# Down projection of a SwiGLU layer on one core: another order of seven- and eight-product pairs, other pieces with their low parts added by DMA, and more lead

## The chip, the cores and the metric

One core of one Trainium2 chip runs the whole layer as one program. The metric is the device time of that program in microseconds (us); lower is better. What a measurement of this kernel can tell from no change is about 0.5%, or 1.45 us.

## The reference

One decoder layer in float32 for 256 tokens of width 1024. Only its last part matters here:

```python
h = rms_norm(x, norm2_g[l])
x = x + (jax.nn.silu(h @ w_gate[l]) * (h @ w_up[l])) @ w_down[l]
```

`w_gate` and `w_up` are 1024 x 2816, `w_down` is 2816 x 1024. Ahead of it stand the input projection, attention over 256 tokens, a causal convolution with its norm, and the output projection.

## The kernel before

**Products in parts.** TensorE multiplies in the rounded type fp32r. To keep float32 accuracy the kernel splits every operand into a high part (the value rounded to fp32r) and a low part (value minus high part), and adds up three products: high by high, low by high, high by low. Each weight therefore needs two preparing steps after it has been loaded. ScalarE copies it into the tile `wh` with rounding (line 265). The low part `wl` comes in one of two ways, in the helper `low_part` (lines 213 to 219): VectorE subtracts (line 219), or, for the pieces in the list `BY_DMA`, ScalarE writes the negated high part into `wl` (line 216) and a DMA issued by GpSimd adds the weight to it from memory (line 217).

**Pieces, blocks and places.** Weights are loaded by SyncE as blocks of 128 x 2048 (1 MB, tiles `raw`, line 196). There are four buffers for blocks. Half a block is a piece of 128 x 1024. There are eight places for pieces (`WGT = 8`, each place one `wh` and one `wl`); a new piece takes the place that holds the piece with the lowest number. The next block is loaded when the last reader of a block in its buffer is through: for ordinary blocks after the low part of their second piece, for the blocks of the down projection as told below.

**Lead.** The program is written out in one order, with `step()` calls that let side tasks emit their next instructions. Every engine takes its instructions strictly in that order. At each point `feed(upto)` (line 252) emits the copies up to one piece beyond `upto`, and the low parts up to `upto`, where `upto` is the piece now being multiplied plus a lead. The lead is `LEAD = 4`, and 5 from piece `FAR = 46` on and in the whole down projection. Copies are emitted in the order `turns`, which is by number but for the pieces in `BEHIND`: `BEHIND = {75: 72, ...}` puts the copy of piece 75 right behind that of piece 72.

**Gate and up.** Pieces 28 to 71 hold `w_gate` and `w_up`, two pieces for each of 22 groups `f` of 128 columns (tiles `fg` and `fu`, lines 292 and 294). `glu_task` computes silu(gate) times up for each group on ScalarE and VectorE and makes the activations for the down projection.

**Down.** The 22 groups make 11 pairs. A pair is a product of (2 x 2 blocks of activations) by (2 x 2 blocks of weights of 128 x 512). A pair marked F in the string `PAIRS` is done with seven block products after Strassen and Winograd, a pair marked P (plain) with eight. The products go to banks named `sum` (line 932, in the helper `add`). A fast pair has three pieces: the first is taken from its block as it is, the second and third are sums of its weights, which VectorE makes with three additions (lines 234 to 236, tiles `t`; the second piece needs the first of them, the third needs all). Its first quarter block is used alone, too: `single` (line 244) splits it with a copy on ScalarE (line 200) and a subtraction on VectorE (line 201), in the tiles `b11h` and `b11l` for every other fast pair and in `other` for the ones between and for the last. `single` of a pair is emitted at the start of the pair ahead of it, and asks for the block four further on. The products with that quarter (`M1`) stand third in a pair, and first in the last fast pair. A plain pair has two pieces, and its block is free after the copies, or, where VectorE makes the low parts, after these. Down pieces have the numbers 72 to 101, blocks the numbers 36 to 46, one for each pair.

The loop over pairs (lines 958 to 975) does pairs 0 to 9 in order; the last pair is done at the end, bank by bank, with the output (lines 1001 to 1009).

Of the kernel before, what the change touches and what calls it, by code (L numbers as in the profile page):

```python
# [36 lines left out]
LEAD = 4  # L37
# [20 lines left out]
V_PIECE = 21  # L58
SS_WAIT = 2
OUT_LATE = 6  # L60
PAIRS = "FFPFFPFFFFP"
FAST = [p for p in range(NF // 2) if PAIRS[p] == "F"]
PLAIN = [p for p in range(NF // 2) if PAIRS[p] == "P"]
DOWN = 72
BEHIND = {75: 72, 78: 74, 83: 79, 86: 82, 88: 85, 94: 90, 97: 93}
BY_DMA = [*range(45, DOWN, 3), 71, *BEHIND]
FAR = 46
SUMS = {66: 0, 69: 1}
FORMS_LATE = 11
# [72 lines left out]
def _build(nc, tc, t, ctx):  # L142
# [10 lines left out]
    def mm_bank(name, cols=512):  # L153
        return psum.tile([P, cols], F32, name=name, tag="mm", bufs=4)

    def t_bank(name, tag="t"):
        return psum.tile([P, 512], F32, name=name, tag=tag, bufs=2)
# [30 lines left out]
    def load_block(i, between=None):  # L188
        if i >= NB:
            return  # L190
        r = raw.tile([P, BW], F32, name=f"raw{i}", tag="raw")
        n = BW // (2 if between else 1)
        for j in range(BW // n):
            if j:
                between()
            nc.sync.dma_start(r[:, j * n:(j + 1) * n], t["w"][i - 2][:, j * n:(j + 1) * n])
        blocks[i] = r
# [5 lines left out]
    def new_piece():  # L203
        j = turns[len(pieces)]
        z = places.index(min(places))
        places[z] = j
        pieces[j] = [wgt.tile([P, PIECE], F32R, name=f"w{s}{j}", tag=f"w{s}{z}") for s in "hl"]
        i, a = divmod(j * PIECE, BW)
        if j >= DOWN:
            return pieces[j], down_piece(*down[j - DOWN]), j  # L210
        return pieces[j], blocks[i][:, a:a + PIECE] if i > 1 else None, j

    def low_part(dst, src, by_dma=False):

        if by_dma:
            nc.scalar.activation(dst[1], dst[0].bitcast(F32), AF.Copy, scale=-1.0)  # L216
            nc.gpsimd.dma_start(dst[1], src.bitcast(F32R), accum_op=ALU.add)  # L217
        else:
            nc.vector.tensor_tensor(dst[1], src, dst[0].bitcast(F32), op=ALU.subtract)  # L219
# [5 lines left out]
    index = {d: DOWN + a for a, d in enumerate(down)}  # L225
    turns = sorted(range(DOWN + len(down)), key=lambda j: BEHIND[j] + 0.5 if j in BEHIND else j)
    wsums, b11 = {}, {}
# [19 lines left out]
    def home(j):  # L247

        i, a = divmod(j * PIECE, BW)
        if j >= DOWN:  # L250
            p, a = down[j - DOWN]
            i, a = DOWN // 2 + p, (a if p in PLAIN else 1) * PIECE
        return t["w"][i - 2][:, a:a + PIECE]
# [7 lines left out]
    def feed(upto, more=1):  # L261
        last = DOWN + len(down) - 1
        while len(pieces) <= min(upto + more, last):
            dst, src, j = new_piece()
            nc.scalar.activation(dst[0], src, AF.Copy)  # L265
            if j in BY_DMA:
                low_part(dst, home(j), True)
            waiting.append((dst, src, j))
            waiting.sort(key=lambda w: w[2])
        while waiting and waiting[0][2] <= upto:  # L270
            dst, src, j = waiting.pop(0)
            if j not in BY_DMA:
                low_part(dst, src)
            if j < DOWN and j % 2:
                load_block(j // 2 + RAW)
            elif j >= DOWN and down[j - DOWN][0] in PLAIN and down[j - DOWN][1]:
                load_block(DOWN // 2 + down[j - DOWN][0] + RAW)
# [19 lines left out]
    def halves(out, bank, side):  # L297

        nc.scalar.activation(side, bank[:, T:], AF.Copy)
        nc.vector.tensor_tensor(out, bank[:, 0:T], side, op=ALU.add)  # L300
# [420 lines left out]
    for h in range(H):  # L721
        if h % 2 == 0:
            step()
        base, pair = (h % 2) * HD, h // 2
# [111 lines left out]
    def glu_task(f, pg, pu):  # L836
        tg = late.tile([P, T], F32, name=f"tg{f}", tag="tg", bufs=2)
        halves(tg, pg, side(f"gs{f}"))
        nc.vector.tensor_tensor(tg, tg, r_bc, op=ALU.mult)
        s = late.tile([P, T], F32, name=f"sf{f}", tag="sf", bufs=2)  # L840
        yield 1
        nc.scalar.activation(s, tg, AF.Silu)  # L842
        yield max(1, ffn["up"][f] - now[0])
        pair, second = divmod(f, 2)
        if pair in PLAIN:
            ac = late.tile([P, T], F32, name=f"ac{f}", tag="ac")
        else:
            q = FAST.index(pair)
            if q not in pair_sums:
                pair_sums[q] = late.tile([P, 9 * P], F32, name=f"ps{q}", tag="ps")  # L850
            ps = pair_sums[q]
            ac = ps[:, 0:T] if second else ps[:, T:2 * T]
        halves(ac, pu, side(f"us{f}"))
        nc.vector.tensor_tensor(ac, ac, s, op=ALU.mult)
        if pair in PLAIN:
            a = 2 * PLAIN.index(pair) + second
            nc.scalar.activation(acts[:, 0, a, :], ac, AF.Copy)
            yield 1
            nc.vector.tensor_tensor(acts[:, 1, a, :], ac, acts[:, 0, a, :].bitcast(F32), op=ALU.subtract)
        elif second:  # L860
            if q == len(FAST) - 1:
                yield FORMS_LATE


            p3 = ps.rearrange("p (b q) -> p b q", q=P)
            nc.vector.tensor_tensor(p3[:, 4:6], p3[:, 2:4], p3[:, 0:2], op=ALU.subtract)
            nc.vector.tensor_tensor(p3[:, 6:8], p3[:, 5:6].to_broadcast([P, 2, P]), p3[:, 2:5:2], op=ALU.subtract)
            nc.vector.tensor_tensor(p3[:, 8], p3[:, 2], p3[:, 3], op=ALU.subtract)
            yield 1
            parts = ((forms[q][:, :, 0:3], p3[:, 0:3]), (forms[q][:, :, 3:7], p3[:, 5:9]))  # L870
            for to, of in parts:
                nc.scalar.activation(to[:, 0], of, AF.Copy)
            yield 1
            for to, of in parts:
                nc.vector.tensor_tensor(to[:, 1], of, to[:, 0].bitcast(F32), op=ALU.subtract)
# [4 lines left out]
    for f in range(NF):  # L880
        pg = t_bank("fg2", "s") if f == 2 else mm_bank(f"fg{f}")
        pu = mm_bank(f"fu{f}") if f < 3 else t_bank(f"fu{f}", "s")
        groups = [[(z, k) for k in range(KT)] for z in range(2)]
        if f == 0:
            groups = [[(z, k) for k in range(4)] for z in range(2)] + [[(z, k) for k in range(4, KT) for z in range(2)]]
        a = 0
        for g, group in enumerate(groups):
            jobs = []
            for z, k in group:
                if a % 4 == 0:  # L890
                    if f == a == 0:
                        step()
                    now_at = (off + a * P) // PIECE
                    if now_at in SUMS and a % 8 == 4:
                        add_up(SUMS[now_at])
                    feed(now_at + LEAD - (f == 0 and a < 12) + (now_at >= FAR))
                    if f or a:
                        step()
                if f and a == KT:
                    spawn(glu_task(f, pg, pu))  # L900
                    ffn["up"][f] = now[0] + 2
                jobs.append((z, (pg, pu)[z], wtile(off + (z * KT + k) * P, P), xg[:, :, k, :]))
                a += 1
            mm2(jobs, [z for z, k in group if k == 0], [z for z, k in group if k == KT - 1])
        if f == NF - 3:
            single(0)
        if f == 0:
            spawn(glu_task(0, pg, pu), GLU0_WAIT)
            ffn["up"][0] = now[0] + GLU0_WAIT
        off += 2 * KT * P  # L910
# [48 lines left out]
    for pair in range(NF // 2 - 1):  # L959
        for q in range(1, len(FAST)):  # L960
            if FAST[q] == pair + 1:
                single(q)
        if pair in PLAIN:
            for a in range(2):
                feed(index[pair, a] + LEAD + 1)
                plain(pair, a, dict(enumerate((M2, N3, N4, C22))))
        else:
            q = FAST.index(pair)
            groups = ((M2, N3, M1), (N5, M7), (M6, N4)) if q < len(FAST) - 1 else ((M1, N5), (M7, M6), (M2, N3, N4))
            for part, ms in enumerate(groups):  # L970
                feed(index[pair, part] + LEAD + 1)
                step()
                for m in ms:
                    seventh(q, m)
# [26 lines left out]
    for z, m in enumerate((M2, N3, N4, "left", "right")):  # L1001
        step()
        i, n = divmod(min(z, 3), 2)
        part = slice(0, W) if z < 3 else slice((z - 3) * T, (z - 2) * T)
# [59 lines left out]
```

## Time and profile before

| | us |
|---|---|
| median of 3 runs | 290.73 (290.6 to 291.97) |
| the profiled execution's own time | 292.5 |
| its span, first to last instruction | 290.7 |
| TensorE busy | 283.4 |
| VectorE busy | 236.2 |
| ScalarE busy | 202.7 |
| GpSimd busy | 44.1 |
| mean granted TensorE clock | 0.992 |

The engines are named PE (TensorE), PEld (its weight loads), DVE (VectorE), ACT (ScalarE), POOL (GpSimd) and SP (SyncE). The page gives busy time for each engine; the list of waits tells who waited for whom; the timeline gives start and length of each instruction, with the idle time before it and what ended that in square brackets. Instructions on one engine overlap a little at their ends, so what an instruction costs in a row of others is the distance of starts, not its length. Times of the timeline count from the span's start.

### The profile page before, as it was taken

What the parts mean: (1) busy time and instruction counts of PE and PEld (TensorE: products, weight loads), DVE (VectorE), ACT (ScalarE), POOL (GpSimd) and SP (SyncE); (2) the same over time, 40 slices, a digit from 0 to 9 for tenths busy, and PEclk for the clock granted to TensorE, in tenths of its full rate; (3) what the DMA queues carried; (4) which work ended last, traced back from release to release, by engine and by line L of the source; (5) the groups of instructions that cost most, each with busy time, mean ns of one, the idle gap of its engine ahead of it and who ended that gap; (6) DMA issues with size and microseconds to landing.
All of it is one profiled execution on the core that took longest, in us unless ns stands there. A gap on an engine that the chain in (4) does not pass through costs nothing.

```text
span 290.7 us, 4120 instructions
## 1 busy us (share of the span) xinstructions
PE 283.4 (97%) x1466; PEld 236.1 (81%) x1466; DVE 236.2 (81%) x420; ACT 202.7 (70%) x331; POOL 44.1 (15%) x71
## 2 busy tenths in 40 slices
PE   8999999999999999999999999999999999999695
PEld 6888877788788888888888888888888888877484
DVE  4979995895976879999779866787796879879975
ACT  5757678996739674666879687778775758668550
POOL 0005474433000000000111111111111011111052
PEclk9999999999999999999999999999999999999979
DMA  6999868647014942564999999979997485986203
GB/s 272 371 422 381 370 216 300 246 145 267 24 43 128 408 145 92 209 252 176 300 229 250 349 294 231 254 248 291 243 267 215 158 216 159 259 213 192 46 0 144
DMA packets 12918, 65.62 MB, mean 226 GB/s; under 512 B 1697, under 2 KB 2305, under 8 KB 7266
## 3 DMA queue, kind: packets, MB, share of 16 engines
q1 hardware_dynamic: 10018, 55.14, 51.6%
q0 software_dynamic: 2736, 10.22, 18.2%
q8 instruction: 11, 0.18, 0.2%
q14 instruction: 9, 0.07, 0.1%
q10 hardware_dynamic: 144, 0.00, 0.0%
HBM read 64.31 MB, written 1.05 MB: 225 GB/s over the span
## 4 chain that ended last, share of the span: by engine, by line
PE 90%; DVE 4%; issue 2%; ACT 1%; DMA 1%; ACTq 0%; DVEq 0%
PE p L709 19%; PE fg L292 14%; PE fu L292 14%; PE sum L932 13%; PE po L755 8%; PE fg L294 7%; PE fu L294 7%; DVE wl L219 1%; DVE t L234 1%; PE S L543 1%; DMA first<-first 1%; PE pT L573 1%; DVE t L235 1%; ACT wh L265 1%; PE O L729 1%
## 5 line engine op out<-in xcount | busy, mean ns | idle before, releaser
L265 ACT ACTIVATE wh<-raw 128x1024 fp32r<-128x1024 f32 x82 | 84.8, 1051 | 3.5 <-DMA raw<-w 3.5
L219 DVE TENSOR_TENSOR wl<-raw,wh 128x1024 fp32r<-128x1024 f32 x65 | 78.4, 1220 | 6.0 <-ACT wh L265 6.0
L292 PE MATMUL fu<-g,wh 128*128 128x512 f32 x176 | 62.5, 395 | 0.0
L292 PE MATMUL fg<-g,wh 128*128 128x512 f32 x176 | 62.4, 394 | 0.0
L294 PE MATMUL fg<-g,wl 128*128 128x256 f32 x176 | 48.8, 277 | 0.0
L294 PE MATMUL fu<-g,wl 128*128 128x256 f32 x176 | 48.8, 277 | 0.0
L217 POOL DMA_DIRECT2D wl<-w x17 | 14.7, 865 | 184.2 <-ACT sf L842 76.6
L292 PEld LDWEIGHTS fg<-g,wh 128*128 128x128 f32 x176 | 33.0, 187 | 7.7
L292 PEld LDWEIGHTS fu<-g,wh 128*128 128x128 f32 x176 | 33.0, 188 | 7.6
L294 PEld LDWEIGHTS fg<-g,wl 128*128 128x128 f32 x176 | 33.1, 188 | 0.0
L294 PEld LDWEIGHTS fu<-g,wl 128*128 128x128 f32 x176 | 33.1, 188 | 0.0
L709 PE MATMUL p<-wh,xh 128*128 128x512 f32 x80 | 26.2, 409 | 0.1
L265 ACT ACTIVATE wh<-t 128x1024 fp32r<-128x1024 f32 x16 | 16.9, 1056 | 13.4 <-DVE t L234 12.3
L932 PE MATMUL sum<-wh,forms 128*128 128x512 f32 x84 | 25.9, 390 | 0.0
L709 PE MATMUL p<-wh,xl 128*128 128x512 f32 x80 | 25.0, 395 | 0.0
L709 PE MATMUL p<-wl,xh 128*128 128x512 f32 x80 | 24.7, 390 | 0.0
L219 DVE TENSOR_TENSOR wl<-t,wh 128x1024 fp32r<-128x1024 f32 x16 | 19.5, 1220 | 1.5 <-ACT wh L265 1.4
L216 ACT ACTIVATE wl<-wh 128x1024 fp32r<-128x1024 f32 x17 | 18.1, 1062 | 0.5
L932 PEld LDWEIGHTS sum<-wh,forms 128*128 128x128 f32 x84 | 15.7, 188 | 3.2
L709 PEld LDWEIGHTS p<-wh,xl 128*128 128x128 f32 x80 | 15.3, 191 | 3.4
L709 PEld LDWEIGHTS p<-wh,xh 128*128 128x128 f32 x80 | 14.5, 191 | 4.3 <-issue 1.0
L709 PEld LDWEIGHTS p<-wl,xh 128*128 128x128 f32 x80 | 15.1, 189 | 3.3
(203 smaller groups left out, 483.2 us busy)
## 6 DMA issues: line engine op xcount, KB each, us to landing
raw<-w SPq DMA_DIRECT2D x44, 1024.0 KB, 6.7
wl<-w POOLq DMA_DIRECT2D x17, 512.0 KB, 8.7
first<-first SPq DMA_DIRECT2D x8, 384.0 KB, 5.2
raw<-w SPq DMA_DIRECT2D x2, 512.0 KB, 6.9
xtok<-xtok SPq DMA_DIRECT2D x2, 512.0 KB, 9.6
x<-xtok SPq DMA_DIRECT2D x2, 512.0 KB, 6.8
c_rows<-rows SPq DMA_DIRECT2D x1, 768.0 KB, 10.5
out<-x SPq DMA_DIRECT2D x3, 256.0 KB, 2.0
```

The costliest lines, as they stand in the source:

```text
L216: nc.scalar.activation(dst[1], dst[0].bitcast(F32), AF.Copy, scale=-1.0)
L217: nc.gpsimd.dma_start(dst[1], src.bitcast(F32R), accum_op=ALU.add)
L219: nc.vector.tensor_tensor(dst[1], src, dst[0].bitcast(F32), op=ALU.subtract)
L234: nc.vector.tensor_tensor(u[:, 0:2 * W], w[:, 0:2 * W], w[:, W:3 * W], op=ALU.add)
L235: nc.vector.tensor_tensor(u[:, 2 * W:3 * W], u[:, 0:W], w[:, 2 * W:3 * W], op=ALU.add)
L265: nc.scalar.activation(dst[0], src, AF.Copy)
L292: nc.tensor.matmul(out.rearrange("p (a q) -> p a q", a=2), w[0], both, start=z in first and z not in seen, stop=False)
L294: nc.tensor.matmul(out[:, 0:T], w[1], both[:, 0, :], start=False, stop=z in last and left[z] == 0)
L543: nc.tensor.matmul(banks[a][:, out], G["qT"][rows, j, q], G["kT"][rows, j, k], start=True, stop=True)
L709: nc.tensor.matmul(banks[i], (xh, xh, xl)[a][:, kt, sls[i]], w[a % 2], start=kt == 0 and a == 0, stop=kt == KT - 1 and a == 1)
L755: nc.tensor.matmul(po[i, n], G["mix"][l][:, k, i * P:(i + 1) * P], w[r], start=k == a == 0, stop=k == KT - 1 and a == 2)
L932: nc.tensor.matmul(banks[m], lhs, rhs, start=first, stop=last)
```

## The change

Four edits. The order of pairs becomes FFFPFFFPFFP. The DMA makes the low parts of the four pieces of the first two plain pairs (81, 82, 92, 93) and no longer of the first pieces of five fast pairs nor of pieces 71, 78 and 86. The copies of those four pieces are put in front of copies of sums: 81 behind 75, 82 behind 78, 92 behind 83, 93 behind 86. The lead from piece 46 on is six instead of five. Besides, the copy of a plain pair's activations is emitted one step later.

```diff
-PAIRS = "FFPFFPFFFFP"
+PAIRS = "FFFPFFFPFFP"
...
-BEHIND = {75: 72, 78: 74, 83: 79, 86: 82, 88: 85, 94: 90, 97: 93}
-BY_DMA = [*range(45, DOWN, 3), 71, *BEHIND]
+BEHIND = {81: 75, 82: 78, 92: 83, 93: 86}
+BY_DMA = [*range(45, DOWN, 3), *BEHIND]
...
             a = 2 * PLAIN.index(pair) + second
+            yield 1
             nc.scalar.activation(acts[:, 0, a, :], ac, AF.Copy)
...
-                    feed(now_at + LEAD - (f == 0 and a < 12) + (now_at >= FAR))
+                    feed(now_at + LEAD - (f == 0 and a < 12) + 2 * (now_at >= FAR))
...
-                feed(index[pair, a] + LEAD + 1)
+                feed(index[pair, a] + LEAD + 2)
...
-                feed(index[pair, part] + LEAD + 1)
+                feed(index[pair, part] + LEAD + 2)
```

Lines behind 856 have a number higher by one in the changed kernel.

How ScalarE's instructions stand at the start of the down projection, before. The number behind `wh` is the piece, that behind `raw` the block, that behind `t` the fast pair whose sum it is (counted from 0); what follows an underscore is an inner number. The rows begin behind the last gate group's instructions; `other` from `ps7` is an activation form that only the last fast pair reads.

```order
L265 ACTIVATE wh83_2557<-raw40_2402 128x1024
L216 ACTIVATE wl83_2558<-wh83_2557 128x1024
L265 ACTIVATE wh80_2574<-raw39_2344 128x1024
L265 ACTIVATE wh81_2587<-t2_2589 128x1024
L265 ACTIVATE wh82_2604<-t2_2589 128x1024
L872 ACTIVATE other_2518<-ps7_2351 128x384
L872 ACTIVATE other_2518<-ps7_2351 128x512
L200 ACTIVATE b11h_1077<-raw39_2344 128x512
L265 ACTIVATE wh86_2620<-raw41_2521 128x1024
L216 ACTIVATE wl86_2621<-wh86_2620 128x1024
L265 ACTIVATE wh84_2640<-t3_2642 128x1024
L200 ACTIVATE other_2518<-raw40_2402 128x512
```

There the copies that stand early (83, 86) read blocks 40 and 41, those of pairs 4 and 5. In the changed kernel the same stretch of ScalarE, up to the quarter of pair 4 (`other` from `raw40`):

```order
L858 ACTIVATE act_1069<-ac21_2547 128x256
L200 ACTIVATE b11h_1077<-raw38_2257 128x512
L265 ACTIVATE wh80_2581<-t2_2562 128x1024
L265 ACTIVATE wh83_2595<-raw40_2403 128x1024
L265 ACTIVATE wh92_2609<-raw43_2598 128x1024
L216 ACTIVATE wl92_2610<-wh92_2609 128x1024
L873 ACTIVATE other_2520<-ps7_2354 128x384
L873 ACTIVATE other_2520<-ps7_2354 128x512
L265 ACTIVATE wh84_2623<-t3_2625 128x1024
L265 ACTIVATE wh85_2642<-t3_2625 128x1024
L265 ACTIVATE wh86_2652<-raw41_2523 128x1024
L200 ACTIVATE other_2520<-raw40_2403 128x512
```

The copy of piece 92 reads block 43, that of pair 7, three blocks beyond the one that the piece ahead of it reads, and stands ahead of the copies of the sums of pair 4 and of its quarter.

In the changed kernel's SyncE queue block 42 goes into the buffer of block 39 and waits for the copy of piece 82 on ScalarE; block 43 goes into the buffer of block 38 and waits for the quarter of pair 2 (`b11l` from `raw38`) on VectorE, since pair 2 is now a fast pair.

VectorE in the changed kernel, from the low part of piece 84 to the quarter of pair 4 and the sums behind it:

```order
L219 TENSOR_TENSOR wl84_2624<-t3_2625,wh84_2623 128x1024
L876 TENSOR_TENSOR other_2520<-ps7_2354,other_2520 128x384
L876 TENSOR_TENSOR other_2520<-ps7_2354,other_2520 128x512
L219 TENSOR_TENSOR wl85_2643<-t3_2625,wh85_2642 128x1024
L219 TENSOR_TENSOR wl86_2653<-raw41_2523,wh86_2652 128x1024
L201 TENSOR_TENSOR other_2520<-raw40_2403,other_2520 128x512
L234 TENSOR_TENSOR t4_2686<-raw41_2523 128x1024
```

Before, the quarter of pair 4 stood there right behind the low part of 84, and two low parts stood behind it:

```order
L219 TENSOR_TENSOR wl84_2641<-t3_2642,wh84_2640 128x1024
L201 TENSOR_TENSOR other_2518<-raw40_2402,other_2518 128x512
L219 TENSOR_TENSOR wl85_2665<-t3_2642,wh85_2664 128x1024
L219 TENSOR_TENSOR wl87_2689<-raw41_2521,wh87_2688 128x1024
L234 TENSOR_TENSOR t4_2702<-raw42_2563 128x1024
```

## The prediction

> **What bounds the kernel now.** I read the page's busy times first, then the list of TensorE's waits.
>
> ```profile
> PE 283.4 (97%) x1466; PEld 236.1 (81%) x1466; DVE 236.2 (81%) x420; ACT 202.7 (70%) x331; POOL 44.1 (15%) x71
> ```
>
> ```profile
> PE sum L932 <- ACT other L200: 2.2, 1, 2.2
> PE sum L932 <- DVE other L201: 0.5, 1, 0.5
> PE sum L932 <- DVE b11l L201: 0.4, 1, 0.4
> ```
>
> TensorE is busy 97% of the span, and all the waits that count are in the down projection (`sum`), each for the high or low part of a quarter block. Next, the stretches of that stage (busy time and, in brackets, instructions of PE, PEld, DVE, ACT, POOL; then granted clock, DMA share, GB/s):
>
> ```profile
> 241.60:256.60 15.00, 15.00 (x68) 12.43 (x67) 13.10 (x15) 11.05 (x12) 1.73 (x2) 1.00 0.90 254
> 256.60:274.95 18.35, 15.23 (x64) 11.31 (x62) 16.37 (x19) 11.62 (x15) 1.72 (x2) 1.00 0.56 137
> 274.95:290.70 15.75, 12.41 (x51) 9.90 (x51) 10.53 (x14) 5.22 (x7) 5.89 (x4) 0.86 0.18 67
> ```
>
> In the middle row VectorE is busy 16.4 of 18.35 us; there it is the bound. In the last the granted clock is 0.86. TensorE's timeline gives the price:
>
> ```profile
> 226.58 0.62 PE L932 MATMUL sum<-wh,forms 128*128 128x512 f32 x2
> ...
> 229.31 0.61 PE L932 MATMUL sum<-wh,forms 128*128 128x512 f32 x2
> ...
> 229.99 0.61 PE L932 MATMUL sum<-wh,forms 128*128 128x512 f32 x2
> ...
> 236.11 1.07 PE L932 MATMUL sum<-wh,act 128*128 128x512 f32 x4
> ...
> 241.55 0.61 PE L932 MATMUL sum<-wh,forms 128*128 128x512 f32 x2
> ...
> 272.41 0.39 PE L932 MATMUL sum<-wl,forms 128*128 128x512 f32 x1
> 274.95 1.32 PE L932 MATMUL sum<-other 128*128 128x512 f32 x3 [2.15 <-ACT other L200]
> ...
> 279.65 0.62 PE L932 MATMUL sum<-wh,other 128*128 128x512 f32 x2
> ...
> 287.08 0.28 PE L932 MATMUL sumright<-wl,act 128*128 128x256 f32 x1
> ```
>
> A block product of three matmuls takes 0.68 us (229.99 - 229.31), one matmul 0.227; so a fast pair needs 7 x 0.68 = 4.76 us, a plain one 5.44 (241.55 - 236.11), and the last pair, done bank by bank, 2 x 4 x 0.68 = 5.44 too. Without any wait the last matmul, of 256 columns (0.11), would start at 226.58 + 8 x 4.76 + 2 x 5.44 + 5.44 - 0.11 = 280.97. It starts at 287.08: 6.1 us are lost. The two short waits are 0.5 and 0.4 in the list; the long one, 272.41 to 274.95 less 0.23, is 2.3; and the twelve matmuls from 274.95 to 279.65 take 4.70 where 12 x 0.227 = 2.72 would do, so 2.0 for the lowered clock behind the wait. That is 5.2; the other 0.9 is restarts and smaller breaks.
>
> **The change part by part.** Prices on VectorE and ScalarE, as distances of starts:
>
> ```profile
> 239.13 0.42 DVE L866 TENSOR_TENSOR ps<-ps 128x256 f32<-128x256 f32 x1
> ...
> 240.13 1.22 DVE L219 TENSOR_TENSOR wl<-t,wh 128x1024 fp32r<-128x1024 f32 x1
> ...
> 241.44 0.69 DVE L201 TENSOR_TENSOR b11l<-raw,b11h 128x512 fp32r<-128x512 f32 x1
> 242.04 1.15 DVE L875 TENSOR_TENSOR other<-ps,other 128x384 fp32r<-128x384 f32 x2
> 243.12 1.22 DVE L234 TENSOR_TENSOR t<-raw 128x1024 f32<-128x1024 f32 x1
> ...
> 251.13 1.22 DVE L234 TENSOR_TENSOR t<-raw 128x1024 f32<-128x1024 f32 x1
> ...
> 253.71 2.50 DVE L219 TENSOR_TENSOR wl<-t,wh 128x1024 fp32r<-128x1024 f32 x2
> ...
> 263.96 1.22 DVE L219 TENSOR_TENSOR wl<-t,wh 128x1024 fp32r<-128x1024 f32 x1
> 265.10 1.22 DVE L234 TENSOR_TENSOR t<-raw 128x1024 f32<-128x1024 f32 x1
> ```
>
> ```profile
> 226.77 0.63 ACT L200 ACTIVATE other<-raw 128x512 fp32r<-128x512 f32 x1 [1.08 <-PE fu L294]
> 227.31 1.05 ACT L265 ACTIVATE wh<-t 128x1024 fp32r<-128x1024 f32 x1
> 228.26 0.40 ACT L842 ACTIVATE sf<-tg 128x256 f32<-128x256 f32 x1
> 228.57 1.05 ACT L265 ACTIVATE wh<-raw 128x1024 fp32r<-128x1024 f32 x1
> 229.52 0.36 ACT L299 ACTIVATE us<-fu 128x256 f32<-128x256 f32 x1
> ...
> 231.15 1.04 ACT L265 ACTIVATE wh<-raw 128x1024 fp32r<-128x1024 f32 x1
> 232.23 1.06 ACT L216 ACTIVATE wl<-wh 128x1024 fp32r<-128x1024 f32 x1
> 233.19 1.04 ACT L265 ACTIVATE wh<-raw 128x1024 fp32r<-128x1024 f32 x1
> ```
>
> Low part 1.14 (265.10 - 263.96), sums of a pair 2.58 (253.71 - 251.13), quarter 0.60 (242.04 - 241.44), the last pair's differences 1.00 (240.13 - 239.13) and their low parts 1.08 (243.12 - 242.04); on ScalarE a copy 0.96, or 1.08 when the negation of the same piece follows, and a negation 0.96.
>
> Who makes the low parts. VectorE gets four more (17 pieces by DMA become 13): 4 x 1.14 = 4.6 us. ScalarE loses four negations, GpSimd four DMA issues; nobody waits for those. A fast pair now takes VectorE 2.58 + 0.60 + 3 x 1.14 = 6.60 us against TensorE's 4.76, where it took 5.46 with one piece by DMA. A plain pair takes VectorE nothing against 5.44. So over FFFP it falls back 3 x 1.84 = 5.5 and regains 5.4, while before it fell back 0.7 a pair over four fast pairs in a row, with the long wait at their end. That wait goes: ahead of the last fast pair now stand a plain and one fast pair.
>
> The copies in front. This is where I expect the gain to be lost. ScalarE comes to the copy of piece 92 when it has done that of 83, and that copy needs block 43. Block 43 can be asked for only when VectorE has the quarter of pair 2. When is that? Before, `us` of the last group starts at 229.52. Now the copy and negation of 82 stand where one copy stood: +1.08. The low parts of 71 and 75, now VectorE's, add 2 x 1.14 = 2.28 ahead of that; two idle spells of VectorE stand in the same stretch:
>
> ```profile
> 223.14 0.42 DVE L300 TENSOR_TENSOR ac<-fu,us 128x256 f32<-128x256 f32 x1 [0.76 <-ACT us L299]
> ...
> 225.46 1.23 DVE L219 TENSOR_TENSOR wl<-t,wh 128x1024 fp32r<-128x1024 f32 x1 [1.44 <-ACT wh L265]
> ```
>
> These can take up to 2.2 of it, but ScalarE waits there for VectorE in turn; I pass 0.7 on, bounds 0 to 2.28, nearer the idle rows. So `us` at 231.3. Then on VectorE: its copy's end 0.4, two activation steps 0.8 (229.91 to 230.71 in the next fence), sums 2.58, low part of 79 1.14, quarter 0.69 with its end: 236.9.
>
> ```profile
> 229.91 0.42 DVE L300 TENSOR_TENSOR ac<-fu,us 128x256 f32<-128x256 f32 x1 [0.29 <-ACT us L299]
> ...
> 230.71 1.22 DVE L219 TENSOR_TENSOR wl<-raw,wh 128x1024 fp32r<-128x1024 f32 x1
> ```
>
> How long a block takes, from two windows of the trace, 226 to 245 and 245 to 262, three blocks each:
>
> ```profile
> DMA to landing us min/median/max: 4.7/5.0/5.3
> ```
>
> ```profile
> DMA to landing us min/median/max: 6.2/7.3/7.4
> ```
>
> Blocks 41 and 42 are asked for some 7 us earlier and the next adding DMA only after the copy of 92, so block 43 travels nearly alone: I take 5.0, bounds 4.7 and 7.4. The Trainium skill's page "DMA: Bandwidth & Descriptors", section "Measured (HBM→SBUF, 128 partitions, SWDGE, issued from GpSimd)", gives 6.15 us for 1 MB by GpSimd's path; these blocks come by SyncE's and the three rows are quicker, and by the page the forecast would be 1.1 us later, 291.5.
>
> So the copy of 92 starts at 241.9, not at about 237 when 83 is done. Behind it on ScalarE stand its negation, two forms, and the copies of 84, 85 and 86 and the quarter of pair 4. The copy of 84 ends after 1.08 + 0.96 + 0.96 (two forms with 896 columns together, priced as one copy of 1024) + 1.05 = 4.05 later, at 246.0. Then VectorE does the low part of 84, the differences' low parts, the low parts of 85 and 86, and the quarter: 1.14 + 1.08 + 2.28 + 0.69 = 5.2, at 251.2. TensorE, unhindered, wants that quarter at 226.58 + 3 x 4.76 + 5.44 (start of pair 4, 246.3) + 2 x 0.68 + 2 x 0.227 = 248.1. A new wait of 3.1 us, in two parts: for the high part (until ScalarE has copied 85, 86 and the quarter, 246.0 + 0.96 + 0.96 + 0.6 = 248.5), and, two matmuls later, for the low part.
>
> From there on VectorE sets the pace. From the quarter of pair 4 to that of pair 8 it has four sums, nine low parts and three quarters: 4 x 2.58 + 9 x 1.14 + 2 x 0.60 + 0.69 = 22.5 us less 0.1 of overlap, ending at 251.2 + 22.4 = 273.6. TensorE, restarted at 251.2, wants it after 0.23 + 4 x 0.68 + 2 x 4.76 + 5.44 + 2 x 0.68 + 0.45 = 19.7, at 270.9: 2.7 us of further waits, parted between the quarters of pairs 6 and 8. If the clock is lowered behind the 3.1 us as it was behind the 2.15, its 2.0 us lie inside these 2.7 and cost nothing; without that cover they would count in full. Behind the quarter of pair 8 (273.6): rest of pair 8 0.23 + 4 x 0.68 = 2.95, pair 9 4.76 (its quarter is ready after 2 x 1.14 + 0.69, at 276.6, wanted at 277.0), last pair 5.44 - 0.11. The last matmul starts at 286.75.
>
> The rest at nothing. One more piece of lead: the eight places stay, so a copy waits for the piece just multiplied; behind it on ScalarE stand only that group's steps, which need later products. The reordered pairs keep 8 fast and 3 plain, the same matmuls. The step between an activation and its copy: the last plain pair's activations are read some 40 us later. The tail behind the last matmul, 290.7 - 287.1 = 3.6 us, stays.
>
> **Sum.** 286.75 against 287.08: -0.3 us, with bounds: landing -0.3 to +2.4, lateness of VectorE -0.7 to +1.6. The profiled execution took 292.5, 1.8 more than its span, and the runs' median is 290.73; I put the difference on the median: 290.4 us, no change. One wait of 2.3 with its clock loss is traded for two others.
>
> **The rivals.** Faster: block 43 is not late. If it is there when ScalarE comes for it, the copy of 84 follows the first sum of pair 3 instead. VectorE, behind the quarter (236.8), does the low part of 80, an activation's low part 0.4, the differences 1.0, the low part of 83 and the first sum 1.22: 241.7; the copy of 84 ends at 242.8 instead of 246.0, so -3.2: 287.2. For it: the order was meant so, and TensorE could gain up to 6.1. Against: the buffer's release stands in the SyncE queue. 0.14.
>
> Slower: block 43 travels as the late ones do. It lands after 7.3 us, and all behind it moves by 2.3: wait at pair 4 of 5.4, time 292.7. This decides from a landing of some 6.8 us (or as much more lateness ahead of it). For it: the second window, and the page's median of 6.7 over all blocks:
>
> ```profile
> raw<-w SPq DMA_DIRECT2D x44, 1024.0 KB, 6.7
> ```
>
> Against: those blocks had company on the queues. 0.22.
>
> The lowered clock lasts longer. Two waits in a row could keep it down twice as long as 4.7 us: 4.0 lost, 2.7 covered, +1.3, so 291.7, within the bound. 0.08. My forecast's own case has 0.56.
>
> **How the numbers follow.** A measurement of this kernel can tell about 0.5%, 1.45 us: below 289.3 and above 292.2. Faster: 0.14, and 0.07 of my own case: with landing and lateness both at their low ends it gives 289.4, and a sum of so many steps is no surer than the 0.1 to the edge. Slower: 0.20 of the slow case and 0.02 of mine. Same: 0.57. The range 289.0 to 292.7 leaves out the faster rival and the upper end of the slower one, 0.2 in all.
>
> **What would show it.** Right: a wait of ScalarE's `wh` for a block of some 4 to 5 us near 237; TensorE's waits for `other` near 249 and 251; VectorE without idle time from about 246 to 277; no wait of TensorE at the last fast pair, and a clock of 1.00 in the last stretch, the dip now near 250. Wrong: TensorE passing 251 without a wait (the faster rival), the landing of that block above 6.8 us (the slower), or waits in the gate and up stage, where I see none.

## The result, and the profile after

| | before | after |
|---|---|---|
| median, 11 runs each on the same chip, us | 291.97 (290.41 to 292.84) | 293.62 (292.94 to 294.96) |
| ratio, 95% interval | | 1.0067 [1.0043, 1.0092] |
| profiled execution: time, span | 292.5, 290.7 | 293.62, 291.8 |
| its mean granted clock | 0.992 | 0.994 |

The change makes the kernel slower by 0.7%, 1.65 us by the medians. The three runs shown first (median 290.73) were quicker than most runs of the kernel before; what the granted clock says of that stands at the experiment e4.

The busy line of the page after. VectorE has risen by 3.7 us, ScalarE has fallen by 4.9, GpSimd by 4.2, TensorE by 1.2:

```profile
PE 282.2 (97%) x1466; PEld 236.1 (81%) x1466; DVE 239.9 (82%) x424; ACT 197.8 (68%) x327; POOL 39.9 (14%) x67
```

TensorE's waits in the down projection after:

```profile
PE sum L933 <- DVE other L201: 2.1, 1, 2.1
PE sum L933 <- ACT other L200: 1.7, 1, 1.7
...
PE sum L933 <- DVE b11l L201: 0.8, 1, 0.8
```

The long wait at the last fast pair (2.2) is gone. In its place stand 1.7 and 2.1, for the high and the low part of one quarter. The same stretches as before, with the same columns:

```profile
241.60:256.60 15.00, 11.29 (x42) 8.58 (x42) 10.80 (x14) 11.24 (x14) 1.72 (x2) 0.89 0.56 150
256.60:274.95 18.35, 17.62 (x78) 14.18 (x76) 18.15 (x21) 10.31 (x12) 0.00 (x0) 1.00 0.36 121
274.95:291.80 16.85, 13.52 (x64) 11.25 (x64) 11.56 (x15) 5.35 (x8) 5.13 (x4) 1.00 0.17 62
```

The granted clock dips in the first row now, not in the last. TensorE is idle for 3.7 of 15 us there, and VectorE, idle for 4.2 of the same 15 us, is then busy for 18.15 of 18.35. TensorE's timeline:

```profile
226.88 0.63 PE L933 MATMUL sum<-wh,forms 128*128 128x512 f32 x2
...
249.82 0.73 PE L933 MATMUL sum<-other,forms 128*128 128x512 f32 x2 [1.66 <-ACT other L200]
252.61 0.80 PE L933 MATMUL sum<-other,forms 128*128 128x512 f32 x1 [2.05 <-DVE other L201]
253.21 1.05 PE L933 MATMUL sum<-wh,forms 128*128 128x512 f32 x2
...
256.35 0.39 PE L933 MATMUL sum<-wl,forms 128*128 128x512 f32 x1
...
274.98 0.50 PE L933 MATMUL sum<-b11l,forms 128*128 128x512 f32 x1 [0.77 <-DVE b11l L201]
...
288.22 0.28 PE L933 MATMUL sumright<-wl,act 128*128 128x256 f32 x1
```

The nine matmuls from 252.61 to 256.35 take 3.74 us where 9 x 0.227 = 2.04 would do: 1.7 for the lowered clock. Why the quarter is late stands on ScalarE: the copy of piece 83, then 5.5 us of waiting for block 43 in the copy of piece 92, and everything else behind that:

```profile
236.78 1.05 ACT L265 ACTIVATE wh<-raw 128x1024 fp32r<-128x1024 f32 x1
243.32 1.06 ACT L265 ACTIVATE wh<-raw 128x1024 fp32r<-128x1024 f32 x1 [5.49 <-DMA raw<-w]
244.41 1.06 ACT L216 ACTIVATE wl<-wh 128x1024 fp32r<-128x1024 f32 x1
```

VectorE shows both ends of it: the quarter of pair 2, for which the load of block 43 waits, and the low part of piece 84 after 4.07 us of idling:

```profile
236.45 0.68 DVE L201 TENSOR_TENSOR b11l<-raw,b11h 128x512 fp32r<-128x512 f32 x1
...
247.39 1.22 DVE L219 TENSOR_TENSOR wl<-t,wh 128x1024 fp32r<-128x1024 f32 x1 [4.07 <-ACT wh L265]
...
251.88 0.68 DVE L201 TENSOR_TENSOR other<-raw,other 128x512 fp32r<-128x512 f32 x1
```

And the DMA view for 236 to 240 us, in which only block 43 is issued (at 237.2). Two queues share the 16 engines: q1 carries the blocks, q0 the adding DMAs. The low part of piece 82, issued at 231.9, moves now; before 236 us its queue carried next to nothing:

```profile
q0 software_dynamic: 139, 0.52, 66.5%
q1 hardware_dynamic: 75, 0.48, 35.5%
issues: line engine op xcount, KB each, median us to landing
raw<-w SPq DMA_DIRECT2D x1, 1024.0 KB, 6.1
```

### The profile page after: what moved, and what is told of

Read it like the earlier page. It is cut to its first block, busy times and chain, and to the rows that moved or that the text cites. A ratio compares the mean times of both kernels' runs of the same rounds, so it can differ in the third digit from the quotient of the medians.

```text
span 291.8 us, 4136 instructions
## 1 busy us (share of the span) xinstructions
PE 282.2 (97%) x1466; PEld 236.1 (81%) x1466; DVE 239.9 (82%) x424; ACT 197.8 (68%) x327; POOL 39.9 (14%) x67
## 4 chain that ended last, share of the span: by engine, by line
PE 87%; DVE 4%; DMA 4%; issue 2%; ACT 1%; SPq 0%; ACTq 0%; DVEq 0%
PE p L709 18%; PE fg L292 14%; PE fu L292 14%; PE sum L933 12%; PE po L755 7%; PE fg L294 7%; PE fu L294 7%; DVE wl L219 2%; DMA raw<-w 2%; DMA first<-first 2%; PE S L543 1%; PE pT L573 1%; ACT wh L265 1%; PE O L729 1%; PE xT L768 1%
## 5 line engine op out<-in xcount | busy, mean ns | idle before, releaser
L219 DVE TENSOR_TENSOR wl<-raw,wh 128x1024 fp32r<-128x1024 f32 x69 | 83.1, 1218 | 3.4 <-ACT wh L265 3.4
L217 POOL DMA_DIRECT2D wl<-w x13 | 11.3, 866 | 173.7 <-PE fu L294 70.5
L933 PE MATMUL sum<-wh,forms 128*128 128x512 f32 x84 | 26.9, 402 | 0.0
L933 PEld LDWEIGHTS sum<-wh,forms 128*128 128x128 f32 x84 | 16.5, 198 | 3.5
L933 PE MATMUL sum<-wl,forms 128*128 128x512 f32 x42 | 16.8, 401 | 0.0
```

The lines of the kernel that those rows point to most:

```text
L933: nc.tensor.matmul(banks[m], lhs, rhs, start=first, stop=last)
```

## The experiments

Theory A: the loss is made by the copy of piece 92, which stands on ScalarE ahead of pair 4's copies and waits there for block 43. Its rivals: the lead, VectorE's additional low parts, or the order of pairs. All ratios are to the kernel before on the same chip, with the 95% interval in brackets; "last matmul" is the start of the last matmul in the run's profile (288.22 in the changed kernel, 287.08 before).

**e1_block_swap: the same kernel, block 43 asked for ahead of block 42.**

```diff
 def single(q):
-        load_block(i + RAW)
+        if q != 2:
+            load_block(i + RAW)
 # feed(), behind the low part of the first plain pair's last piece
+                if down[j - DOWN][0] == PLAIN[0]:
+                    load_block(DOWN // 2 + FAST[2] + RAW)
```

> The changed kernel with one thing undone: block 43 is asked for ahead of block 42, so that it goes into the buffer of block 39 and waits only for the copy of piece 82. Nothing else moves. Theory A (the late block 43 holds ScalarE, and all behind it is late): block 43 is asked for at about 231 instead of 237.2 and is there by 237 when ScalarE has done the copy of 83; ScalarE's 5.5 us wait for a block goes, the two waits of TensorE at pair 4 (1.7 and 2.1) shrink to under 0.6 together, waits of about 1.4 remain at the quarters of pairs 6 and 8 each, and the span falls by about 4 us against the changed kernel (291.8 to about 287.5), so about 3 us (1.1%) under the kernel before. Rival B (VectorE has too much to do, whoever comes late): the two waits only move to later pairs and the span stays within 1 us of 291.8.

Measured: 289.03 us, ratio 0.9912 [0.9883, 0.9942]; last matmul 284.02. TensorE's waits, where only these two are left of those in the down projection:

```profile
PE sum L936 <- DVE other L201: 0.8, 1, 0.8
...
PE sum L936 <- DVE b11l L201: 0.8, 1, 0.8
```

ScalarE's wait for block 43 is 0.7 us; block 42, now asked for at 237.1, holds nobody. The same copies in the same order, the same lead and the same low parts, and the kernel is faster than both. What costs is that one load behind that one copy.

**e5_92_behind_84: the other end of the same wait.**

```diff
-BEHIND = {81: 75, 82: 78, 92: 83, 93: 86}
+BEHIND = {81: 75, 82: 78, 92: 84, 93: 86}
```

> The changed kernel with one number altered: the copy of piece 92 stands on ScalarE behind the copy of 84 instead of in front of it. Blocks are asked for as in the changed kernel. Theory A (the loss is the copy of 84 standing behind a copy that waits for block 43): the copy of 84 now waits only for VectorE's first sum, some 3 us ahead of the landing at 243.3; ScalarE's wait for block 43 shrinks from 5.5 us to about 1; the waits of TensorE near 249 and 252 shrink from 1.7 + 2.1 to about 1.5 together; last matmul between 284.1 and 284.7 instead of 288.2, ratio to the kernel before about 0.993. Rival B (the six pieces of lead, or the choice of pieces whose low parts VectorE makes, carry the loss): last matmul within 0.5 us of 288.2, ratio about 1.006.

Measured: 290.18 us, ratio 0.9943 [0.9921, 0.9965]; last matmul 285.46; ScalarE's wait for block 43 is 1.06 us, TensorE's waits near 249 are 0.4 and 0.8. The waits near 249 came as theory A has it. The last matmul is 0.8 later than the range I gave: block 43 took 6.6 us here, and VectorE's pace leaves waits of 0.8 near 261 and 272. So the cause holds, the size was too good.

**e9_no_add_82: is it the company of the adding DMA that makes block 43 late?**

```diff
-            nc.gpsimd.dma_start(dst[1], src.bitcast(F32R), accum_op=ALU.add)
+            if src is not None:
+                nc.gpsimd.dma_start(dst[1], src.bitcast(F32R), accum_op=ALU.add)
...
-                low_part(dst, home(j), True)
+                low_part(dst, home(j) if j != 82 else None, True)
```

> The changed kernel without one adding DMA: the low part of piece 82 stays the negated high part, so that part of the weight is left out of the products; all else stays. In the changed kernel that DMA is issued at 231.9 and lands 8.6 us later, on top of block 43 (237.2 to 243.3). Theory A (this company makes block 43 take 6.1 us where the prediction took 5.0): block 43 lands in 4.7 to 5.3 us, ScalarE's wait for it shrinks from 5.5 to about 4.4, the last matmul starts 0.8 to 1.3 us earlier than 288.2, ratio about 1.003. Rival (block 42 ahead of it in the queue, which landed after 8.1 us, or its size alone sets the 6.1): block 43 within 0.3 us of 6.1, last matmul within 0.3 of 288.2, ratio about 1.007.

Measured: 291.79 us, ratio 0.9996 [0.9976, 1.0016]; last matmul 286.31. The DMA view of its stretch 235 to 240 us, and ScalarE's copy of piece 92:

```profile
issues: line engine op xcount, KB each, median us to landing
raw<-w SPq DMA_DIRECT2D x1, 1024.0 KB, 4.7
```

```profile
241.42 1.06 ACT L266 ACTIVATE wh<-raw 128x1024 fp32r<-128x1024 f32 x1 [4.16 <-DMA raw<-w]
```

The block lands in 4.7 us instead of 6.1. The DMA views of one us each, starting 1.4 us behind the block's issue, show what held it: in the changed kernel (238.6 to 239.6) the adding DMA's queue moves nearly all,

```profile
q0 software_dynamic: 52, 0.19, 95.2%
q1 hardware_dynamic: 6, 0.05, 19.4%
```

and in e9 (238 to 239) block 43 has the engines for itself:

```profile
q1 hardware_dynamic: 33, 0.27, 68.0%
```

Block 42 lands at 238.7 in the changed kernel and at 236.4 in e9, so e9 takes away the company of block 42 too. But in the changed kernel only 0.03 MB moved on the blocks' queue in the first half us behind the issue of block 43 and next to nothing in the 1.5 us after that, so that block 42 itself can have taken little of the time. The last matmul comes 1.9 earlier, more than expected, since here the down projection also starts 0.6 earlier (226.31 against 226.88); from that start it is 60.0 us against 61.3. With the block landing in 4.7 us, a little sooner than the 5.0 of the prediction, the changed kernel can't be told from the kernel before.

**e2_lead_five: the changed kernel with the lead of before.**

```diff
-                    feed(now_at + LEAD - (f == 0 and a < 12) + 2 * (now_at >= FAR))
+                    feed(now_at + LEAD - (f == 0 and a < 12) + (now_at >= FAR))
-                feed(index[pair, a] + LEAD + 2)
+                feed(index[pair, a] + LEAD + 1)
-                feed(index[pair, part] + LEAD + 2)
+                feed(index[pair, part] + LEAD + 1)
```

> The changed kernel with the lead of five pieces again. Theory A: the copy of 92 is emitted behind more of pair 4's work, so ScalarE's wait for block 43 shrinks from 5.5 to under 2.5 us and stands where less is behind it; TensorE's waits in the down stage add up to some 3 us, none over 1.3, and the time is about 3 us under the kernel before (ratio about 0.99). Rival B: with less lead VectorE is later at every pair, TensorE's waits grow, and the time is not under that of the changed kernel (ratio 1.005 or more). If the sixth piece of lead is needed for what the change gains, B's side is to be seen here too.

Measured: 290.9 us (289.98 to 292.58), ratio 0.9992 [0.9968, 1.0016]; last matmul 284.16. ScalarE's wait for the block is 2.0 us, and no wait of TensorE is above 0.7. The matmuls end about 3 us under those of the kernel before, as expected, the kernel doesn't: its last output step on VectorE starts 1.13 us behind the last matmul (285.29), against 0.32 in the changed kernel. VectorE's last low part and the first step of the output behind it, and the GpSimd addition beside the low part:

```profile
276.46 2.31 DVE L219 TENSOR_TENSOR wl<-raw,wh 128x1024 fp32r<-128x1024 f32 x1
278.69 0.68 DVE L994 TENSOR_TENSOR rest<-sum,rest 128x512 f32<-128x512 f32 x1
```

```profile
276.37 1.32 POOL L985 TENSOR_TENSOR x<-x,rest 128x512 f32<-128x512 f32 x1 [25.96 <-ACT rest L984]
```

A low part takes 1.22 elsewhere (247.39 in the changed kernel); here 2.31, so it took 1.1 us longer, and the steps behind it came later by as much.

**e11_lead_five_x11: that GpSimd step done by VectorE.**

```diff
-    beside(x11, s, m1, r0)
+    onto(x11, m1, r0)
```

> e2_lead_five with one step of the tail moved from ScalarE and GpSimd to VectorE: the first output quarter gets its bank M1 by one VectorE instruction instead of a ScalarE copy and a GpSimd addition. In e2 the last low part took 2.31 us on VectorE beside that GpSimd addition (1.32 us) where 1.22 is usual, and the final steps were late by 0.8 to 1.0 us. If the two engines held each other up there: the low part is back at 1.2, the final steps follow the last matmul at 0.3 us as in the other kernels, the span ends 0.5 to 1.0 us earlier than e2's, and the runs spread less than e2's 2.6 us; ratio about 0.995. Rival (VectorE is late there from its own load): final steps as late as in e2, ratio about 0.999.

Measured: 290.03 us (289.48 to 290.37), ratio 0.9935 [0.9908, 0.9962]; span 287.7 against 288.8. Each of the last low parts takes its usual time again (two in 2.35), and the spread is 0.9 us in 5 runs, where e2 had 2.6 in 12 on another chip. Only 0.4 of the 1.1 us come from the tail (last step 0.68 behind the last matmul), the other 0.7 from an earlier last matmul (283.47), for which I have no cause. So the two engines did hold each other up, and that is part of e2's missing gain; how large a part the runs do not show.

**e3_copies_in_order: the four copies' places.** Pieces 92 and 93 are copied in the order of their numbers, still with low parts by DMA.

```diff
-BEHIND = {81: 75, 82: 78, 92: 83, 93: 86}
-BY_DMA = [*range(45, DOWN, 3), *BEHIND]
+BEHIND = {81: 75, 82: 78}
+BY_DMA = [*range(45, DOWN, 3), *BEHIND, 92, 93]
```

> The changed kernel with the copies of pieces 92 and 93 in number order, their low parts still by DMA. Theory A: ScalarE does not wait for block 43 near 237; but the pieces of pair 4 now compete with nothing and VectorE still has the same work, so some waits of TensorE remain (about 2 and 1 at pair 4, where the order on VectorE is unchanged, and about 2 at the first use of piece 92's low part near 267, since the DMA starts late). Span about 290 to 290.5, 1.5 us under the changed kernel. Rival B: the same waits as in the changed kernel, span 291.5 or more.

Measured: 294.02 us, ratio 1.0086 [1.0058, 1.0115]; last matmul 289.25, span 292.9. The gain expected isn't there, though the waits are near those expected. ScalarE's wait for block 43 is gone, but the adding DMAs of 92 and 93 are now issued at 259.3 and 261.8, land 6.3 and 8.9 us later, and TensorE waits:

```profile
PE sum L933 <- DMA wl<-w: 2.2, 1, 2.2
PE sum L933 <- ACT other L200: 1.4, 1, 1.4
PE sum L933 <- DVE other L201: 0.8, 1, 0.8
```

What the expectation left out is the lowered clock behind them. The mean clock is 0.89 from 241.6 to 256.6 us and 0.91 from 256.6 to 275; nine matmuls from 250.34 on take 3.75 us instead of 2.04, and ten from 270.80 on 3.97 instead of 2.27, so 1.7 us are lost each time. And pair 4's quarter is late for another reason than block 43: it stands behind the copy of a sum that waits 3.2 us for TensorE to finish with a place:

```profile
247.21 1.06 ACT L265 ACTIVATE wh<-t 128x1024 fp32r<-128x1024 f32 x1 [3.19 <-PE sum L933]
248.17 0.61 ACT L200 ACTIVATE other<-raw 128x512 fp32r<-128x512 f32 x1
```

So the early copy bought something: the adding DMA has to be early. Taking the copies back cures the wait for block 43 and brings two others.

**e6, e7, e12: the order and the lead by themselves, on the kernel before.** The diffs: for e6 the order with piece 89 for 88 in the list, for e7 the lead, for e12 both.

```diff
# e6 and e12
-PAIRS = "FFPFFPFFFFP"
+PAIRS = "FFFPFFFPFFP"
-BEHIND = {75: 72, 78: 74, 83: 79, 86: 82, 88: 85, 94: 90, 97: 93}
+BEHIND = {75: 72, 78: 74, 83: 79, 86: 82, 89: 85, 94: 90, 97: 93}
# e7 and e12
-                    feed(now_at + LEAD - (f == 0 and a < 12) + (now_at >= FAR))
+                    feed(now_at + LEAD - (f == 0 and a < 12) + 2 * (now_at >= FAR))
-                feed(index[pair, a] + LEAD + 1)
+                feed(index[pair, a] + LEAD + 2)
-                feed(index[pair, part] + LEAD + 1)
+                feed(index[pair, part] + LEAD + 2)
```

> The kernel before with the new order of pairs alone; its list of pieces with low parts by DMA stays, but 89 stands there for 88, since in the new order 88 is a sum and 89 is the first piece of a fast pair. Lead five. Theory A (the order gives the gain of some 4 us, and the copies in front take it away): no copy of ScalarE waits for block 43 ahead of pair 4's sums; the 2.15 us wait and the lowered clock behind it are gone; about 1.2 us of waits near 258 and under 0.5 near 248 and 273; last matmul at about 283.1, ratio about 0.988. Rival (the order itself brings the waits at pairs 4 and 6, whoever makes the low parts): waits of 2 us or more between 248 and 262, last matmul at 286 or later, ratio 0.998 or above.

> The kernel before with the lead of six pieces alone. Theory A (the lead is dear only together with the copies in front): VectorE makes low parts one piece earlier and the long waits of the old order stay: one near 251 of up to 1.8 us, one near 278 of about 2.2 us; last matmul between 287.4 and 288.6 against 287.1, ratio 1.001 to 1.006. Rival (the lead is the step that helps): the wait of 2.15 us gone, ratio 0.995 or less. Rival B (the lead alone carries the loss of the change): ratio 1.006 or above with a wait of ScalarE for a block of several us.

> e6_order_alone with the lead of six pieces: the new order and the lead together, without the copies in front and with the old choice of low parts by DMA. e6 gave 0.989, the lead alone 1.011. If the two simply add, ratio about 1.000 and last matmul about 286.1. Theory (the lead puts more low parts ahead of each quarter on VectorE, and the plain pairs of the new order give part of that back): waits of 0.8 to 1.5 us near 239, 255 and 261, none over 2, last matmul between 285 and 287, ratio 0.996 to 1.002. Rival (the lead was dear only in the old order, because of its four fast pairs in a row): last matmul within 0.7 of e6's 282.96, ratio 0.992 or less; then the copies in front carry the whole loss.

| | time, us | ratio | last matmul |
|---|---|---|---|
| e6, order | 288.61 | 0.9894 [0.9863, 0.9925] | 282.96 |
| e7, lead | 295.21 | 1.011 [1.0073, 1.0147] | 290.24 |
| e12, both | 291.8 | 1.002 [1.0004, 1.0036] | 286.73 |

The order alone leaves one wait of 0.8 (for an adding DMA) and one of 0.2. The lead alone is dearer than I put it. It keeps the wait at the last fast pair and adds others, for quarters which on ScalarE and VectorE now stand behind more copies and low parts:

```profile
PE sum L932 <- ACT other L200: 2.0, 1, 2.0
PE sum L932 <- DVE other L201: 1.5, 1, 1.5
PE sum L932 <- DMA wl<-w: 0.9, 1, 0.9
...
PE sum L932 <- DVE b11l L201: 0.5, 1, 0.5
PE sum L932 <- ACT b11h L200: 0.4, 1, 0.4
```

Order and lead add up: 0.9894 x 1.011 = 1.0003 against 1.002. So the change's gain of 3 us is in its first edit, and beside the old list of low parts the lead gives that back, though no copy waits for a block. This price belongs to the old list: e1 has the same order and the same lead with the new list and the copies in front, and is at 0.9912, near the 0.9894 of the order with lead five. The loss of the changed kernel is therefore not the lead's by itself. The lead five beside e1's other edits was not run.

**e8_swap_m1_97: the best version.** e1 with the quarter wanted later and one low part less on VectorE.

```diff
-            groups = ((M2, N3, M1), (N5, M7), (M6, N4)) if q < len(FAST) - 1 else ((M1, N5), (M7, M6), (M2, N3, N4))
+            groups = ((M2, N3), (N5, M7, M1), (M6, N4)) if q < len(FAST) - 1 else ((M1, N5), (M7, M6), (M2, N3, N4))
-BEHIND = {81: 75, 82: 78, 92: 83, 93: 86}
+BEHIND = {81: 75, 82: 78, 92: 83, 93: 86, 97: 94}
```

> e1_block_swap with two more edits: the products with the quarter block (M1) stand fifth in a fast pair instead of third, so TensorE wants the quarter 1.4 us later; and piece 97 gets its low part by DMA (its copy behind 94), which takes 1.14 us from VectorE ahead of the last fast pair. If what is left in e1 (waits of 0.8 near 259 and 0.8 near 271) is VectorE's pace with the quarter wanted too early: the wait near 271 goes, the one near 259 stays at about 1, last matmul at about 282.4 against 284.0, ratio about 0.986. Rival (the two waits only move into later products, and the new adding DMA lands late as in e3): last matmul 284 or later, ratio 0.991 or more.

Measured: 287.97 us, ratio 0.9872 [0.9846, 0.9897]; last matmul 282.42, as expected, 1.5 above the 280.87 without any wait (for that figure see the end of step one below). Waits of 0.7 near 258 and 0.4 near 273 are left.

**e10_order_82: fewer low parts on VectorE under the new order.**

```diff
# against e6
-BEHIND = {75: 72, 78: 74, 83: 79, 86: 82, 89: 85, 94: 90, 97: 93}
+BEHIND = {75: 72, 78: 75, 81: 77, 82: 79, 83: 80, 86: 84, 89: 85, 94: 90, 97: 93}
```

> The kernel before with the new order of pairs, lead five, and another list of pieces with low parts by DMA: {75: 72, 78: 75, 81: 77, 82: 79, 83: 80, 86: 84, 89: 85, 94: 90, 97: 93}; so the first pieces of the fast pairs and the two pieces of the first plain pair, none of the second. If what e6 left (0.8 and 0.2 us of waits, last matmul 282.96) is VectorE's pace, two low parts less on VectorE bring the last matmul to about 281.6, near the 280.97 without any wait, ratio about 0.984. Rival (more adding DMAs meet the blocks, as in e3): a wait of TensorE for an adding DMA or of ScalarE for a block of over 2 us, last matmul 283 or later, ratio 0.989 or more.

Measured: 289.28 us, ratio 0.9921 [0.989, 0.9951]; last matmul 283.89. The rival holds. An adding DMA issued at 237.1 shares the queues with two blocks, lands 9.9 us later, and is the one wait that counts:

```profile
PE sum L932 <- DMA wl<-w: 2.3, 1, 2.3
```

**e4_before_again: the kernel before, once more.** No edit.

> The kernel before once more, for its profile and the spread of its times, which lie at 290.4 to 291.1 and at 292.0 to 292.8. Theory C: the two groups are executions without and with the lowered clock behind the 2.15 us wait, whose price in the profile was 2.0 us; then the executions with the higher granted clock are the shorter ones, by about 2 us. Rival: the groups come from the start of the program (loads of the first blocks), and the granted clock tells nothing.

Measured: 291.96 us (290.5 to 292.57), ratio 0.9998 [0.9974, 1.0021]; last matmul 286.94. With it, 87 runs of the kernel before have a granted clock on record: 56 have 0.994 or less and a median of 292.25; 31 have 0.998 or more and a median of 290.84. So the granted clock does tell the runs apart, and theory C has the direction right: the medians lie 1.4 us apart, where 2.0 was expected, and the two groups overlap a little (290.76 to 292.96 and 290.36 to 291.52). Only profiled runs show where the clock was low; that it was behind the wait of some 2.15 us in the others too is inferred. All 11 runs of the changed kernel have 0.994 or less. In e9, 6 runs at 0.994 or less have a median of 291.70, 4 at 1.00 have 291.91: there it costs nothing that these ten runs could show.

## Why the prediction was wrong

**What held.** The order alone is worth what the first part of the argument says: the long wait with its clock loss goes, and e6 is 3 us faster. ScalarE waits at the copy of 92 near 237 (I put 4 to 5 us, it was 5.5). The quarter of pair 2 ended at 237.1 (236.9). TensorE waits near 249 and 251. VectorE is without idle time from 247.4 to 280. TensorE does not wait at the last fast pair, and the clock is 1.00 in the last stretch; the dip came near 254.

**Step one that failed: the landing of block 43, taken as 5.0 us because it "travels nearly alone".** It took 6.1. I looked for the next adding DMA and forgot the one before: that of piece 82, issued 5.3 us ahead of the block and landing 3.3 us behind the block's issue. Without it the block takes 4.7 (e9). The down projection also began 0.3 later (226.88 against 226.58); TensorE's profile has two waits near the start of the program, 0.5 us at 4.6 and 0.6 at 8.3, that the profile before does not have. All that follows moved by the two together, 1.4: the quarter of pair 4 ended at 252.6 (251.2), that of pair 8 at 274.9 (273.6). 286.75 + 1.1 + 0.3 = 288.15; the last matmul started at 288.22. Two sums of the prediction have a slip: the last matmul's 0.11 is written in both but not taken off, and their terms add up to 280.87 and 286.64, not 280.97 and 286.75. The difference to the kernel before would have been -0.4 instead of -0.3, so nothing hangs on it. The Trainium skill's page "DMA: Bandwidth & Descriptors", section "Measured (HBM→SBUF, 128 partitions, SWDGE, issued from GpSimd)", has 6.15 us for 1 MB. It counts the time in which the DMA engines are busy, the traces here count from issue to landing, so the two are not quite the same thing. The 6.1 is close to it, but the same block took 4.7 in e9 and 6.6 in e5, so here the nearness belongs to the company that block 43 had.

**Step two: the base, "I put the difference on the median: 290.4".** The sum was made against the profiled execution (292.5), in which the clock was lowered for 2.0 us. By their times, 290.6 and 290.73, two of the three runs behind the median were probably of the kind in which it isn't (the 56 runs with a lowered clock took 290.76 or more; the clock of these three is not on record): they had nothing of that 2.0 to win back. That these three fell so was chance; the median of 11 runs is 291.97. In the changed kernel VectorE sets the pace behind the wait, so a run without a lowered clock would hardly be quicker, as in e9; none of its runs was one. The profiled executions compare like with like, 293.62 - 292.5 = 1.1, which is the 1.14 between their last matmuls, 0.3 of it the later start. On the profiled base the forecast was 292.2; the 1.8 us between the bases, 1.1 for the landing and 0.3 for the start make the whole error of 3.2.

**Covered clock loss.** The sum said that 2.0 us of lowered clock would lie inside 2.7 of waits. It was 1.7 inside 2.5 (1.7 + 0.77), and e9's two groups of runs agree that it costs nothing. What I did not draw from it: such a loss stays covered in every run, and the one that the change removes had been there only in about two runs of three (56 of 87).

**The lead.** I wrote "One more piece of lead" under the rest at nothing. Since the sum followed the program's own order, the low parts of 85 and 86 ahead of the quarter were in it, and the total didn't suffer. But as a price of the edit it was wrong: 1.1% alone (e7). And that behind a waiting copy stand "only that group's steps" does not hold in general: in e3 the quarter of pair 4 stands behind such a copy.

**The rivals.** The slower one's mechanism was the one that came, at half its size: 6.1 lies between my 5.0 and the 6.8 from which it was to decide; on the wrong base even its 292.7 was too low. The faster rival, block 43 not late, is what e1 makes: its price, 3.2 us off the last matmul's 286.75, gives 283.55, and e1 has 284.02.

**Open.** The medians differ by 1.65 us. With the kernel before at its lowered-clock median (292.25) 1.4 are left, of which the two traces show 1.1 and 0.3 of that is the start. Seven of the changed kernel's runs show a clock of 0.988 where its profile shows 0.994; whether that is a second dip, and where, was not profiled.

## What to carry to other kernels

An instruction moved forward on an in-order engine brings its wait along: price it by the landing of what it reads, and look for transfers that were issued before it and are still moving, not only for those to come. Price each edit of a bundle alone and in its company: here the order held the gain, the lead lost 1.1% beside one list of pieces, but with the other list and the block in time that loss was not there (e1), and the copies in front lost as long as one block came late. And before a difference worked out in one profiled execution is put on a median, ask whether the runs behind that median have the stall that the change removes.

## What was not expected of the hardware

- The lowered clock comes behind waits of about 2 us, taken together, and not always. In the profiles it follows the wait of 2.15 us before, those of 1.66 + 2.05 in the changed kernel, the 2.06 of e9 and also 1.44 + 0.77 with two matmuls between in e3; behind the 2.33 of e10 the clock stays at 1.00 (247 to 252 us). By the mean clock of all runs, 56 of 87 runs of the kernel before are at 0.994 or less, 6 of 10 in e9, 2 of 6 in e10. Nine of ten runs of e12, with waits up to 1.2 us in its profile, and all of e5 (up to 0.8) are at 0.998 or more.
- VectorE and GpSimd hold each other up when both read from SBUF: in e2 a low part took 2.31 us beside an addition on GpSimd that started 0.1 us earlier; in e10 the addition took 2.07 us, not 1.3, where the low part had started first. The Trainium skill's page "SBUF — State Buffer", section "Who interferes with whom", says that a VectorE instruction with two inputs in SBUF contends with a GpSimd instruction that reads SBUF, and that the order of issue decides which of the two is held. Both traces agree.
- The landing of a 512 KB adding DMA goes from 5.4 to 9.9 us within e10, above the 6.7 that was the median of a 1 MB block before.
